# Two edits to the hand-set order of a streaming encoder layer: how many weight chunks may be split ahead at the end of the first feed-forward, and how many due pieces may run between two products in linear memory's heads

## The chip, the cores and the metric

The kernel runs on one core of a Trainium2 chip. The metric is the device time of one execution in microseconds (us); lower is better. The engines are named as in the profile: PE is TensorE (PEld its weight loads), DVE is VectorE, ACT is ScalarE, POOL is GpSimd, SP is SyncE, which issues most transfers.

## The reference

One layer of an encoder on 576 tokens: 512 of a new stream and 64 that continue a running one. D = 1024, feed-forward width 2816, four heads of matrix memory ("linear memory", mLSTM) of width 256, sixteen attention heads of width 64. All of it in f32.

```python
h = LN1(alpha*x + 0.5*FFN1(x))            # FFN: (silu(x@w_gate) * (x@w_up)) @ w_down
z = h @ w_in  -> mLSTM q,k,v,o,i,f | attention q,k,v | gates g_m, g_a
h = LN2(alpha*h + w_out(sig(g_m)*P_m(mLSTM(h)) + sig(g_a)*P_a(BandAttn(h))))
y = LN3(alpha*h + 0.5*FFN2(h))
# one mLSTM chunk, per head:
s   = (q k^T) * exp(dmat - m_t)
num = w_inter * (q C) + s v
h   = num / max(|w_inter * (q n) + sum(s)|, exp(-m_t))
C'  = decay*C + (w_s*k)^T v               # state; h is then normalised and gated by sig(o)
```

## The kernel before, in words

**Products.** Activations lie as 128 rows (features) by 576 columns (tokens), eight tiles for D. A weight chunk is 128 x 1024 f32: eight 128 x 128 blocks, one for each k tile. For f32 accuracy every operand is split into a rounded high part and a low part (the rest), and a product is three matmuls: wh·xh, wh·xl, wl·xh (`mm`, L132, is the one place where matmuls are issued; `transpose` is L142). The columns are taken in two halves. The `up`/`gate` products, most of the down product and the input projections run in a seven-product (Strassen-like) form; it is not touched here.

**Splitting a weight chunk.** `pump` loads a chunk into a raw buffer `wr` (two of them; SP, L246), copies it rounded on ACT into `wh` (`act`, L146) and subtracts on DVE into `wl` (`tt`, L149). There are four `wh` and four `wl` buffers (`NWB = 4`). The raw buffer comes free when the subtraction is done; a `wh`/`wl` pair comes free when the last matmul of its chunk is done. The chunks ("in",48), ("in",40) and ("in",32) are split in two pieces of 512 columns each. `plan` holds the order of all chunks; `take` marks the next chunk as in use (and splits it at once, if that has not happened), `done` gives it back. `pump` splits chunk c while c < taken + limit and while fewer than four chunks are split and not given back; it loads up to c + 1. `limit` is 2.

**The order of PE.** PE's instruction order is the order of the program text. A small queue, `Order`, puts the side work into it: `later(dt, fn)` enters a piece with a due time on a clock that advances with the estimated length of each matmul, and `tick`, called after each k step of a large product (three matmuls), runs every piece that is due. The calls of `pump` come from this queue too. The queues of ACT, DVE, POOL and SP are filled by the framework's scheduler: an instruction that is ready goes by its place in the program text, and `hot(n)` / `high_priority(offset=n)` moves it n places ahead. Each engine then runs its queue strictly in order.

**End of the first feed-forward** (`ffn`, n = 1). The last chunks of the plan are the seven-product chunks of output tiles 6 and 7, then four plain chunks: tile 6 with k 0 to 7 and with k 16 to 21, tile 7 with the same two (`plain`; called 6a, 6b, 7a, 7b below). They make the second column half (B) of tiles 6 and 7. Then come ("in",48), ("in",40), ("in",32), "if" (attention v, k, q of the first head pair and the memory's gate rows; called V0, K0, Q0, IF below) in one `gemm` with the passes `WAVE_M`: V0, K0 and Q0 together for the first half, IF for the first half, then the same for the second half. So the first k step of it needs three chunks split. Its right-hand side is the output of the layer norm `ln1`: `stats` (sums over features on PE: six narrow matmuls, one wide, six narrow; then `rsqrt` on POOL L491 and `dg` on DVE), `centre` (eight subtractions of the mean, `s<-s,c`, six on DVE, two on POOL), `spread` (one matmul, `aux<-dg,one`) and `apply` for each k tile (a scale on DVE L152, bias and rounding on ACT L146, low part on DVE L149), once for each half. `stats` of the first half is due while 6a runs, that of the second half soon after the `WAVE_M` product has begun.

**Linear memory's heads.** For each head `ml_kq` runs four projection chunks (k, k, q, q, with the causal convolution behind each) and enters the side work; `ml_early` enters the five score pieces (`weights`), `ml_late` the two `state` pieces, the five `hidden` pieces, `norm` and the two `back` transposes. So a head's pieces run between the k steps of the next head's projections, and those of the last head between four gate chunks (`FILL`). `turn5` transposes k or v (five transposes into two PSUM banks). v of the next head may only be turned when all five `hidden` pieces of this one have run; until then its piece enters itself again:

```python
            def v_turn(vf, sink):
                if hid[0] < 5 * h:
                    later(300, lambda: v_turn(vf, sink))
                else:
                    turn5(vf, sink)
```

All side work shares four PSUM banks with the tag `aux`. After the last head `od.drain()` runs what is left in the queue, one piece after the other, and the next products (`gate(7)`, then the projection `mp`) follow.

Of the kernel before, what the change touches and what calls it, by code (L numbers as in the profile page):

```python
# [45 lines left out]
class Order:  # L46


    def __init__(self):
        self.now = 0.0  # L50
        self.heap = []
        self.seq = 0
        self.bg = deque()
        self.bg_t = 0.0

    def later(self, dt, fn):
        self.seq += 1
        heapq.heappush(self.heap, (self.now + dt, self.seq, fn))
# [6 lines left out]
    def tick(self):  # L65
        while self.heap and self.heap[0][0] <= self.now:
            self.pop()
        while self.bg and self.bg_t <= self.now:
            self.bg_t = self.now + self.bg[0][0]
            if next(self.bg[0][1], self) is self:  # L70
                self.bg.popleft()
# [14 lines left out]
def tile_layer(ctx: ExitStack, tc: tile.TileContext, ins, outs):  # L86
# [3 lines left out]
    od = Order()  # L90
# [11 lines left out]
    def hot(off):  # L102
        def wrap(fn):
            def run(*a, **k):
                with tc.high_priority(offset=off):
                    return fn(*a, **k)
            return run
        return wrap

    def nm(s):  # L110
        uid[0] += 1
        return f"{s}_{uid[0]}"
# [11 lines left out]
    def f(ap):  # L124
        return ap.bitcast(F32)
# [19 lines left out]
    def act(out, in_, func=AF.Copy, **kw):  # L145
        return ACT.activation(out, in_, func, **kw)  # L146

    def tt(out, a, b, op, eng=None):
        return (eng or DVE).tensor_tensor(out, a, b, op=op)  # L149
# [18 lines left out]
    NWB = 4  # L168
# [15 lines left out]
    GR = 2150  # L184
    L_MEAN, L_STATS, L_SPREAD, L_SPREAD1 = 300, 1440, 4920, 3600
    plan = []
    wst = {"dma": 0, "conv": 0, "taken": 0, "used": 0, "stop": 0}
    raws, parts = {}, {}
    k0a, added = [], {}

    def add_lo(lo, hi, src):
        act(lo, f(hi), scale=-1.0)
        return POOL.dma_start(lo, src, accum_op=ALU.add)  # L193
# [31 lines left out]
        parts[c] = (hi, lo)  # L225

    @hot(30)
    def pump(limit=2):
        while True:
            c = wst["conv"]  # L230
            if wst["dma"] < len(plan) and plan[wst["dma"]][0] in EARLY + EARLY1:
                wst["dma"] += 1
                continue
            if c < len(plan) and plan[c][0] in EARLY + EARLY1:
                if c not in parts:
                    return
                wst["conv"] += 1
                continue
            if wst["dma"] < min(len(plan), c + 2):
                i = wst["dma"]  # L240
                if plan[i][1] is None:
                    wst["dma"] += 1
                    continue
                raws[i] = wpool.tile([P, 1024], F32, tag="wr", name=nm("wr"), bufs=2)
                src = plan[i][1]
                wst["load"] = SP.dma_start(raws[i][:, :src.shape[1]], src)  # L246
                wst["dma"] += 1
                continue
            if c < wst["stop"] and plan[c][0][0][:2] == "ds" and c < wst["taken"] + 4 and wst["used"] < NWB:
                split_ds(c)  # L250
                wst["used"] += 1
                wst["conv"] += 1
                continue
            if c < wst["stop"] and plan[c][0][0][:2] != "ds" and c < wst["taken"] + limit and wst["used"] < NWB:
                raw = raws.pop(c)
                n = plan[c][1].shape[1]
                hi = wpool.tile([P, 1024], F32R, tag="wh", name=nm("wh"), bufs=NWB)
                if plan[c][0] == "if":

                    r3 = raw[:, :n].rearrange("p (k c) -> p k c", c=64)  # L260
                    h3 = hi.rearrange("p (k c) -> p k c", c=P)
                    act(h3[:, :, 0:64], r3)
                    tt(h3[:, :, 64:128], r3, f(h3[:, :, 0:64]), ALU.subtract)
                    parts[c] = (hi, None)
                else:
                    lo = wpool.tile([P, 1024], F32R, tag="wl", name=nm("wl"), bufs=NWB)
                    step = n if plan[c][0] not in PIECES else 512
                    for a in range(0, n, step):

                        with tc.issue_after(k0a[0].ins) if plan[c][0] == ("in", 50) else nullcontext():  # L270
                            act(hi[:, a:a + step], raw[:, a:a + step])
                        if plan[c][0] in ADDED:
                            added[plan[c][0]] = add_lo(lo, hi, plan[c][1])
                            continue
                        before = wst.pop("behind", None)
                        with tc.issue_after(before.ins) if before is not None else nullcontext():
                            wst["lo"] = tt(lo[:, a:a + step], raw[:, a:a + step], f(hi[:, a:a + step]), ALU.subtract)
                    parts[c] = (hi, lo)
                wst["used"] += 1
                wst["conv"] += 1  # L280
                continue
            return

    def take(key):
        c = wst["taken"]
        assert plan[c][0] == key, (plan[c][0], key)
        wst["taken"] += 1
        if wst["conv"] <= c:
            pump(1)
        assert c in parts  # L290
        later(300, pump)
        return c
# [773 lines left out]
    def plain(n, ts_, hp, cs=(0, 2)):  # L1066

        for c in cs:
            k0, nk = DC[c]
            ids = {t: take((f"dn{n}", t, c)) for t, _ in ts_}  # L1070
            for i in range(nk):
                ww = slice(i * P, (i + 1) * P)
                for t, banks in ts_:
                    wh, wl = parts[ids[t]]
                    for ps, cc, new in banks:
                        xh, xl = hp.get(k0 + i, 0)
                        for w, x in ((wh, xh), (wh, xl), (wl, xh)):
                            mm(ps, w[:, ww], x[:, cc], new and k0 + i == 0 and w is wh and x is xh,
                               c == 2 and i == nk - 1 and w is wl, skip_group_check=True)
                    od.tick()  # L1080
            for t, _ in ts_:
                done(ids[t])
# [42 lines left out]
    def ffn(xs, n, gi, raw, final=None, prev=None):  # L1125
        hh = {}
        with tc.tile_pool(name=nm("hr"), bufs=FT, side="right", reuse_waits="tile") as hr, \
# [80 lines left out]
            with tc.tile_pool(name=nm("h1"), bufs=n1, side="right", reuse_waits="tile") as h1, \  # L1208
# [60 lines left out]
                if n == 1:  # L1269
                    ln.spread_at = L_SPREAD1  # L1270
                    for j in (6, 7):
                        ln.whole(j)
                    Y, V, W = bank()[:, :HT_], bank()[:, :HT_], bank("mm")[:, :HT_]
                    plain(n, ((6, ((Y, A, True),)),), hp_)
                    plain(n, ((7, ((V, A, True),)),), hp_)
                    ln.take(7, A, V, ALU.add)
                    Y, Z = seven(n, 6, inner, ln, Y)
                    ln.take(6, A, Y, ALU.add)
                    ln.last(6, A)
                    ln.last(7, A)  # L1280
                    plain(n, ((6, ((Z, B, False),)),), hp_)
                    ln.take(6, B, Z, ALU.add)
                    ln.last(6, B)
                    plain(n, ((7, ((W, B, True),)),), hp_)
                    ln.take(7, B, W, ALU.add)
                    ln.last(7, B)
                    HALVES[:] = HALVES_[0]
                else:
                    for hf in range(2):
                        ln.residual(6, hf)  # L1290
                    for j, hl in [(j, (hf,)) for hf in (0, 1) for j in (6, 7)]:
                        gemm([[((f"dn{n}", j, c), nk) for c, (_, nk) in enumerate(DC)]], hp_, [ln.cb(j)], (((0,), hl),))
# [94 lines left out]
    def out_cb(t, key, j):  # L1387
        def cb(hf, ps):
            with tc.issue_after(k0a[0].ins) if j == 1 and key == "v" else nullcontext():
                act(hs(t, hf), ps)  # L1390
            if hf == 1:
                SP.dma_start(outs[key][:, j, :], t)
        return cb
# [258 lines left out]
    for i, key in enumerate(EARLY1):  # L1652
        later(9000 + 4000 * i, lambda key=key: early(e1, key, EARLY1))
    gemm([[(("in", 48), KT)], [(("in", 40), KT)], [(("in", 32), KT)], [("if", KT)]], H,
         [out_cb(vf0, "v", 0), out_cb(kf0, "k", 0), q0_cb, gate_cb], WAVE_M)
    for i in range(4):
        combos.last = combos.add(i)
    ln1.close()
# [434 lines left out]
    def gate(j, pool, tag, func=AF.Copy):  # L2093
        s = sg[j] = slot(F32, pool, tag)
        gemm(one(("in", 56 + j)), H, [lambda hf, ps, s=s: act(hs(s, hf), ps, func)])

    for h in range(4):
        st = ml_kq(h)
        ml_early(h, st)
        ml_late(h, st)  # L2100
        for c in FILL[h]:
            gate(c - 56, *((sgp, "sg") if c < 60 else (None, "s")))
    del st
    od.drain()
    SP.dma_start(outs["conv"], conv_st)
    mstack.close()
# [150 lines left out]
```

## Time and profile before

| | |
|---|---|
| median of 3 runs | 1563.21 us (1562.77 to 1563.87) |
| profiled execution: its own time | 1562.92 us |
| profiled execution: span from first to last instruction | 1561.2 us |
| PE busy | 1542.1 us (99%) |
| DVE busy | 1144.0 us (73%) |
| ACT busy | 903.6 us (58%) |
| POOL busy | 206.3 us (13%) |
| mean granted TensorE clock | 0.995 |
| DMA | 208.13 MB, mean 133 GB/s |

The span is divided into stages in the order of the text: the first feed-forward until about 395 us, input projections until about 524 us, attention, then the heads of linear memory from about 859 to 1048 us, the projections and the second feed-forward. In the rows of the profile a number in brackets is the idle time of the engine just before an instruction, with what ended it; "x5" is five instructions of one kind that were merged into one row. `s` is the tag of most activation tiles, `c` the mean of a layer norm.

### The profile page before, as it was taken

How to read it: one execution, taken by the hardware profiler on the slowest of the kernel's cores; microseconds unless marked ns; L12 is line 12 of the kernel's file. 1: busy time of each engine (PE TensorE's matmuls, PEld its weight loads, DVE VectorE, ACT ScalarE, POOL GpSimd, SP SyncE). 2: the span in 40 equal slices, each digit the busy share in tenths (PEclk: the TensorE clock that was granted, in tenths of full speed). 3: DMA queues.
4: the chain of work that ended last, by engine and by line, in shares of the span. 5: the costliest groups of instructions: out<-in, count | busy, mean ns of one | idle time of the engine just before them, and what ended most of it. 6: DMA issues, size and time to landing. Idle time of an engine off the chain costs nothing.

```text
span 1561.2 us, 29480 instructions
## 1 busy us (share of the span) xinstructions
PE 1542.1 (99%) x11615; PEld 1526.5 (98%) x11615; DVE 1144.0 (73%) x2206; ACT 903.6 (58%) x1686; POOL 206.3 (13%) x391
## 2 busy tenths in 40 slices
PE   9999999999899999999999999999999999999998
PEld 9999999999899999999999999999999999999997
DVE  7777778686888677667686666755776777788766
ACT  7545457333766587777864877753456554557333
POOL 2000000000200143433201222202111000001000
PEclk9999999999899999999999999999999999999999
DMA  9322324533664376666534764643665222226334
GB/s 269 113 103 87 103 87 93 145 103 112 182 166 158 107 181 146 154 162 149 125 123 149 189 151 110 176 132 106 187 152 137 97 93 98 92 70 145 119 112 149
DMA packets 77731, 208.13 MB, mean 133 GB/s; under 512 B 8600, under 2 KB 20504, under 8 KB 77592
## 3 DMA queue, kind: packets, MB, share of 16 engines
q1 hardware_dynamic: 61464, 162.40, 31.3%
q0 software_dynamic: 12960, 38.02, 14.3%
q10 hardware_dynamic: 3168, 5.83, 1.1%
q8 instruction: 91, 1.49, 0.4%
q14 instruction: 48, 0.39, 0.1%
HBM read 174.56 MB, written 19.86 MB: 125 GB/s over the span
## 4 chain that ended last, share of the span: by engine, by line
PE 86%; DVE 5%; ACT 4%; DMA 2%; issue 1%; POOL 0%; SPq 0%; DVEq 0%; POOLq 0%; ACTq 0%
PE mm L132 71%; PE aux L132 14%; PE aux L142 2%; DVE s L149 1%; DVE sc L1530 1%; ACT wh L146 1%; DVE s L152 1%; ACT sc L146 0%; DMA wr<-in_w_dn 0%; ACT L146 0%; DVE wl L149 0%; DVE U L152 0%; DMA wr<-in_w_gu 0%; DMA w<-in_w_gu 0%; DMA s<-h 0%
## 5 line engine op out<-in xcount | busy, mean ns | idle before, releaser
L132 PE MATMUL mm<-s,wh 128*128 128x288 f32 (+2 forms) x3757 | 769.6, 298 | 2.3 <-ACT wh L146 1.0
L132 PEld LDWEIGHTS mm<-s,wh 128*128 128x128 f32 x3757 | 604.9, 190 | 5.2 <-ACT wh L146 1.2
L132 PE MATMUL mm<-s,wl 128*128 128x288 f32 (+2 forms) x1854 | 549.2, 296 | 3.4 <-DVE wl L149 3.4
L132 PEld LDWEIGHTS mm<-s,wl 128*128 128x128 f32 x1854 | 350.9, 189 | 3.6 <-DVE wl L149 3.6
L146 ACT ACTIVATE wh<-wr 128x1024 fp32r<-128x1024 f32 (+2 forms) x141 | 140.9, 1006 | 170.6 <-PE mm L132 101.0
L149 DVE TENSOR_TENSOR wl<-wr,wh 128x1024 fp32r<-128x1024 f32 (+2 forms) x95 | 109.9, 1165 | 51.3 <-ACT wh L146 51.2
L132 PE MATMUL mm<-tx,wh 128*128 128x288 f32 x635 | 131.3, 296 | 0.0
L132 PEld LDWEIGHTS mm<-tx,wh 128*128 128x128 f32 x635 | 102.2, 188 | 0.1
L149 DVE TENSOR_TENSOR wl<-wt,wh 128x1024 fp32r<-128x1024 f32 x48 | 58.7, 1224 | 52.8 <-ACT wh L841 52.8
L841 ACT ACTIVATE wh<-wt 128x1024 fp32r<-128x1024 f32 x48 | 50.8, 1059 | 80.2 <-DVE wt L149 79.2
L132 PE MATMUL mm<-tx,wl 128*128 128x288 f32 x326 | 96.1, 295 | 0.0
L149 DVE TENSOR_TENSOR wl<-wu,wh 128x1024 fp32r<-128x1024 f32 x60 | 73.4, 1223 | 28.9 <-ACT wh L841 28.9
L841 ACT ACTIVATE wh<-wu 128x1024 fp32r<-128x1024 f32 x60 | 63.4, 1057 | 36.2 <-PE mm L132 33.0
L132 PE MATMUL mm<-tx,ah 128*128 128x288 f32 x392 | 80.5, 297 | 0.0
L193 POOL DMA_DIRECT2D s<-s x16 | 13.7, 854 | 466.3 <-DVE hb L149 423.6
L146 ACT ACTIVATE h<-h 128x288 f32<-128x288 f32 x78 | 34.0, 436 | 59.9 <-DVE h L149 59.8
L132 PEld LDWEIGHTS mm<-tx,ah 128*128 128x128 f32 x392 | 62.4, 188 | 0.7 <-ACT c L146 0.4
L132 PE MATMUL mm<-h,wh 128*128 128x288 f32 (+2 forms) x304 | 62.7, 296 | 0.1
L149 DVE TENSOR_TENSOR wl<-ws,wh 128x1024 fp32r<-128x1024 f32 x48 | 58.5, 1219 | 4.0 <-ACT wh L841 4.0
L132 PEld LDWEIGHTS mm<-tx,wl 128*128 128x128 f32 x326 | 61.2, 188 | 0.0
L149 DVE TENSOR_TENSOR ws<-wu 128x1024 f32<-128x1024 f32 (+1 forms) x52 | 61.0, 1173 | 0.0
L132 PE MATMUL mm<-tx,al 128*128 128x288 f32 x196 | 57.6, 294 | 0.0
(394 smaller groups left out, 3488.0 us busy)
## 6 DMA issues: line engine op xcount, KB each, us to landing
wu<-in_w_gu SPq DMA_DIRECT2D x78, 512.0 KB, 4.3
wr<-in_w_in SPq DMA_DIRECT2D x54, 512.0 KB, 4.1
wl<-in_w_in POOLq DMA_DIRECT2D x42, 512.0 KB, 6.1
wr<-in_w_dn SPq DMA_DIRECT2D x38, 512.0 KB, 4.0
wu<-in_w_in SPq DMA_DIRECT2D x18, 512.0 KB, 4.8
wr<-in_w_dn SPq DMA_DIRECT2D x20, 384.0 KB, 3.7
s<-s POOLq DMA_DIRECT2D x16, 288.0 KB, 4.1
wu<-in_w_ap SPq DMA_DIRECT2D x8, 512.0 KB, 4.6
```

The lines of the kernel that those rows point to most:

```text
L132: PE.matmul(out, lhsT, rhs, start=start, stop=stop, **kw)
L142: PE.transpose(out, in_, idn)
L146: return ACT.activation(out, in_, func, **kw)
L149: return (eng or DVE).tensor_tensor(out, a, b, op=op)
L152: return DVE.scalar_tensor_tensor(out=out, in0=a, scalar=s, in1=b, op0=op0, op1=op1)
L193: return POOL.dma_start(lo, src, accum_op=ALU.add)
L841: self.last = ACT.activation(hi, src, AF.Copy)
L1530: DVE.tensor_tensor_reduce(out=out, in0=ps, in1=g, op0=ALU.add, op1=ALU.max, scale=1.0, scalar=-3e38, accum_out=acc)
```

## The change

`wst["ahead"]` takes the place of the constant 2 as `pump`'s limit. It is 2 everywhere except from the second column half of tile 6 in the first feed-forward (6a) until the `WAVE_M` product has been issued; there it is `NWB`, which is 4. And `Order` gets a switch, `single`: while it is set (the four heads, not the drain behind them), `tick` runs one due piece and leaves the rest to the next k steps. The earliest due piece goes first. Calls of `pump` and the repeated entries of `v_turn` count as pieces.

```diff
 class Order:
...
+        self.single = False
...
     def tick(self):
         while self.heap and self.heap[0][0] <= self.now:
             self.pop()
+            if self.single:
+                break
...
-    wst = {"dma": 0, "conv": 0, "taken": 0, "used": 0, "stop": 0}
+    wst = {"ahead": 2, "dma": 0, "conv": 0, "taken": 0, "used": 0, "stop": 0}
...
-    def pump(limit=2):
+    def pump(limit=None):
+        limit = limit or wst["ahead"]
         while True:
...
                     ln.take(6, A, Y, ALU.add)
                     ln.last(6, A)
                     ln.last(7, A)
+                    wst["ahead"] = NWB
                     plain(n, ((6, ((Z, B, False),)),), hp_)
...
     gemm([[(("in", 48), KT)], [(("in", 40), KT)], [(("in", 32), KT)], [("if", KT)]], H,
          [out_cb(vf0, "v", 0), out_cb(kf0, "k", 0), q0_cb, gate_cb], WAVE_M)
+    wst["ahead"] = 2
...
+    od.single = True
     for h in range(4):
         st = ml_kq(h)
         ml_early(h, st)
         ml_late(h, st)
         for c in FILL[h]:
             gate(c - 56, *((sgp, "sg") if c < 60 else (None, "s")))
     del st
+    od.single = False
     od.drain()
```

## The prediction

> **What bounds the kernel now.** First the page: the span, the engines, the granted clock.
>
> ```profile
> span 1561.2 us, 29480 instructions
> PE 1542.1 (99%) x11615; PEld 1526.5 (98%) x11615; DVE 1144.0 (73%) x2206; ACT 903.6 (58%) x1686; POOL 206.3 (13%) x391
> PEclk9999999999899999999999999999999999999999
> ```
>
> PE is busy for all but 19 us, so an edit of order can gain only where PE waits or runs slowly. One slice of forty, the eleventh (390 to 429 us), has a lowered clock. Next the waits of PE, over the span (total, times, longest):
>
> ```profile
> PE mm L132 <- DVE wl L149: 3.4, 1, 3.4
> PE aux L142 <- ACT hf L146: 1.8, 2, 0.9
> PE mm L132 <- ACT wh L146: 1.0, 1, 1.0
> PE aux L132 <- DVE og L152: 0.3, 1, 0.3
> ```
>
> Rows one and three are single waits for a weight split; two and four lie in the heads. The window view places them (length; busy time of PE, PEld, DVE, ACT, POOL with counts; clock; DMA):
>
> ```profile
> 396.00:398.00 2.00, 0.50 (x2) 0.30 (x2) 0.70 (x3) 2.00 (x5) 0.84 (x3) 1.00 1.06 379
> ...
> 402.00:404.00 2.00, 2.00 (x10) 1.86 (x9) 0.79 (x3) 0.00 (x0) 0.00 (x0) 0.50 0.73 254
> 404.00:406.00 2.00, 2.00 (x10) 1.86 (x9) 0.17 (x2) 0.79 (x3) 0.00 (x0) 0.50 0.64 252
> 406.00:408.00 2.00, 2.00 (x12) 2.00 (x11) 1.44 (x3) 1.94 (x5) 1.92 (x3) 0.50 0.05 18
> ...
> 410.00:412.00 2.00, 2.00 (x17) 1.89 (x16) 1.63 (x5) 0.58 (x1) 0.86 (x1) 1.00 0.93 234
> ```
>
> So at the first feed-forward's end PE waits 1.0 + 3.4 = 4.4 us, and then runs at half clock for some 8 us. The timeline says why, and how slow:
>
> ```profile
> 386.15 1.03 DVE L149 TENSOR_TENSOR dg<-ident,rs 128x256 f32<-128x256 f32 x1 [0.78 <-POOL rs L491]
> 386.26 1.16 ACT L146 ACTIVATE wh<-wr 128x512 fp32r<-128x512 f32 x2 [1.45 <-PE mm L132]
> ...
> 387.79 1.92 DVE L149 TENSOR_TENSOR s<-s,c 128x288 f32<-128x288 f32 x5
> ...
> 390.60 0.68 DVE L149 TENSOR_TENSOR wl<-wr,wh 128x512 fp32r<-128x512 f32 x1
> ...
> 391.31 0.33 SPq L246 DMA_DIRECT2D wr<-in_w_in  x1
> ...
> 394.63 0.40 PE L132 MATMUL mm<-s,wh 128*128 128x256 f32 x2
> ...
> 395.81 0.63 ACT L146 ACTIVATE wh<-wr 128x512 fp32r<-128x512 f32 x1 [1.70 <-DMA wr<-in_w_in]
> ...
> 399.68 0.68 DVE L149 TENSOR_TENSOR wl<-wr,wh 128x512 fp32r<-128x512 f32 x1
> ...
> 400.42 0.58 PE L132 MATMUL mm<-s,wl 128*128 128x256 f32 x1 [3.42 <-DVE wl L149]
> ...
> 407.52 0.63 PE L132 MATMUL mm<-s,wh 128*128 128x256 f32 x2
> 408.16 0.63 PE L132 MATMUL mm<-s,wh 128*128 128x256 f32 x2
> ...
> 409.27 0.40 PE L132 MATMUL mm<-s,wh 128*128 128x256 f32 x2
> ...
> 409.62 0.40 PE L132 MATMUL mm<-s,wh 128*128 128x256 f32 x2
> ```
>
> Read it backwards. PE, which began the three-chunk product at 394.63, stood until 400.42 for Q0's first low part (DVE, 399.68). Its high part was made at 395.81, when the load landed; from the high part (396.44) to the low part 3.2 us went by, in which DVE did layer-norm work queued ahead of it. The load went out at 391.31, the moment V0's second low part (390.60) gave the raw buffer back; and that stood behind the mean subtractions (387.79), though V0's high parts were done by 387.42. So a chain of three things is late: V0's low part, Q0's load, Q0's low part. Three matmuls of a k step take 0.64 us at half clock (407.52 to 408.16) and 0.35 us at full, from 409 on.
>
> **Part one, `ahead`.** It adds and removes no instruction and no byte; it changes where the text of the splits and loads stands. With limit 2, V0 is entered when 7a starts, K0 when 7b starts, Q0 when the product itself takes it. With limit 4 and four buffers, V0 is entered when 6a is given back, K0 when 6b is, Q0 when 7a is, IF when 7b is: each about one plain chunk sooner in the text. What that moves, chunk by chunk:
>
> 7a, 7b: entered sooner, but there are still four buffers and two raw ones; 0.
>
> V0's high part already runs at the instant that 6a's buffer is free (386.26, released by PE): 0. Its low part is now entered a few instructions after `centre`, within `pump`'s 30 places, so it can go ahead of the mean subtractions: at best as soon as `dg` is done and DVE turns to them, 387.8, and 1.9 us sooner than now. If only some of them are passed, 1 us. I take 1 to 1.9.
>
> Q0's load follows it: 389.4 to 390.3 in place of 391.31. The load took 395.81 - 391.31 = 4.5 us, so it lands at 393.9 to 394.8. One high and one low part (0.63, 0.68) then end at 395.2 to 396.1. PE wants the low part at 394.63 + 0.35 + 0.35 + 0.24 = 395.6. That leaves 0 to 0.5 us of the 4.4, if DVE takes the low part when it is ready. The text place of Q0 now lies ahead of the last `apply` steps; in the run it lay behind them.
>
> Price of passing: the subtractions that are passed start 1.3 us later (two low parts of 0.68). DVE does the same work in either order; if K0's low parts pass too, the first normalised k tile is late. Now it is just in time:
>
> ```profile
> 394.00 0.44 DVE L149 TENSOR_TENSOR s<-s,s 128x288 fp32r<-128x288 f32 x1
> ```
>
> It ends at 394.44, PE needs it at 394.75. A pair of low parts ahead of it would cost 1.0 us of waiting. This is what is late next: the layer norm on DVE. Its bound on the gain: from 394 to 412 the windows above show DVE idle for 1.30 + 1.21 + 1.83 + 0.56 + 0.37 = 5.3 us (it is full in those left out), and the second half has this slack:
>
> ```profile
> 414.24 0.82 DVE L149 TENSOR_TENSOR s<-s,s 128x288 fp32r<-128x288 f32 x2
> 416.64 0.31 PE L132 MATMUL mm<-s,wl 128*128 128x320 f32 x1
> ```
>
> Its first tile is done at 414.65, PE takes it up at 416.6: 2.0 us. With no idle DVE left, PE can reach the second half 7.3 us sooner, not more.
>
> The clock. PE resumed at 400.42 and was slow until some 409.0 (a k step that begins at 408.16 is slow, one at 409.27 is not), 8.6 us. In it lay the norm's sums, which took 3.4 us; the first half's, at full clock, took 1.8:
>
> ```profile
> 402.08 1.27 PE L132 MATMUL aux<-onec,s 128*128 128x1 f32 x6
> ...
> 405.45 0.77 PE L132 MATMUL mm<-s,wh 128*128 128x256 f32 x2
> ...
> 382.65 0.80 PE L132 MATMUL aux<-onec,s 128*128 128x1 f32 x6
> ...
> 384.46 0.51 PE L132 MATMUL mm<-hb,wh 128*128 128x288 f32 x2
> ```
>
> Loss: 1.6 on the sums and (8.6 - 3.4) x (1 - 0.35/0.64) = 2.4 on the rest, 4.0 us. It goes only if no long wait remains: waits of 0.9 us in the heads (below) stand in windows with clock 1.00.
>
> [...]
>
> So part one: at most 4.4 + 4.0 = 8.4 us, capped by DVE at 7.3. The norm keeps DVE waiting for POOL for some of that (0.78 us before `dg` in the first half, 386.15). I take 7.3 - 0.8 = 6.5 us; ends 0 and 8.4. SP: the loads of Q0 and IF may pass the `wu` loads that stand between them; `wu` is first used by the column products behind this stage, so that is covered.
>
> **Part two, `single`.** Same instructions again; PE's order changes. The two windows that hold most of the heads' idle time, and one of the waits:
>
> ```profile
> 880.00:910.00 30.00, 28.96 (x223) 28.20 (x223) 21.38 (x49) 25.21 (x59) 7.09 (x20) 1.00 0.75 197
> ...
> 985.00:1010.00 25.00, 24.04 (x193) 23.55 (x192) 17.92 (x54) 18.83 (x46) 5.97 (x17) 1.00 0.51 132
> ...
> 907.30 0.60 PE L142 MATMUL aux<-ident,qf 128*128 128x128 f32 x4
> 908.81 0.30 PE L142 MATMUL aux<-ident,qf 128*64 128x128 f32 x1 [0.91 <-ACT hf L146]
> ```
>
> With the 0.3 us that PE waits for `og`, 1.04 + 0.96 + 0.3 = 2.3 us. The stall at 908.81 ends a burst (last `hidden`, v turn, k turn, nothing between) that needed its fifth `aux` bank before ACT had emptied the first. With a k step (0.36 to 0.44 us) between the pieces two steps cover 0.8 of 0.91. I take 0.7 for each of the two such bursts and 0.1 of the third wait: 1.5 us; ends +2.3 and, for new waits that nothing here shows, -1.
>
> Delays that it adds: a piece waits one or two k steps, up to 0.9 us. `pump` waits too, but here splits wait for buffers, not for their text:
>
> ```profile
> ACT wh L146 <- PE mm L132: 13.5, 9, 3.4
> ```
>
> At the end of the heads the last `hidden` piece reaches ACT, the output is normalised on DVE (until 1046.72) and transposed on PE, 0.9 us later, so one or two steps are covered there.
>
> ```profile
> 1040.55 0.38 ACT L146 ACTIVATE hf<-aux 64x258 f32<-64x258 f32 x1 [1.57 <-PE aux L132]
> ...
> 1045.02 1.70 DVE L156 TENSOR_SCALAR hf<-hf,mv,mrs 128x256 f32<-128x256 f32 x5
> ...
> 1047.63 1.25 PE L142 MATMUL aux<-ident,hf 128*128 128x128 f32 x10
> ```
>
> Sum: 6.5 + 1.5 = 8.0 us off the profiled execution's 1562.92, 1554.9. The median of the runs is 0.29 above that execution: 1555.2.
>
> **Rivals.** (a) The stall shrinks but the clock still falls. If V0's low part stays behind the subtractions, Q0's load still lands at 395.75; high and low part end at 397.1, PE waits 1.5 us for them and about 1 us more for k tiles that ACT and DVE put behind. Of the 4.4 us 2.6 stay, and with them the 4.0: gain 1.8 + 1.5, 1559.9. For it: PE lost the clock at a time when it had been idle, but for two matmuls, only since 395.5. Against: V0's text passes `centre`.
>
> (b) It does not do what it says. V0 and K0 already wait for buffers, and a queue orders by readiness first, so the order on DVE could stay. Part two alone: 1561.7. Against: the 3.2 us that Q0's low part spent queued are order alone.
>
> (c) Slower, by part two. A `v_turn` that may not run enters itself again every 300 ns, and now each try takes the only place of a k step, so real pieces fall behind while it tries. If the last head's `hidden` pieces slip into the drain, no product covers the chain from the last of them to the transposes, 1040.55 to 1047.63, 7.1 us, and 4.0 us of half clock follow: 1563.2 - 6.5 + 11.1 = 1568. It turns the sign once the slip exceeds 0.9 us of slack by more than part one brings. Against: behind the last head no v waits, and 64 k steps stand for some 25 pieces.
>
> **How the numbers follow.** Forecast 0.64, own range 1553.6 to 1557.9 (part one 5.3 to 7.3, part two 0 to 2.3); (a) 0.16; (b) 0.12; (c) 0.08. The range takes in (a) with up to 1 us of new waits in the heads, and at the low end the full 8.4 + 2.3 = 10.7 us, should DVE not cap it: 1552 to 1561. It leaves out (b) and (c). No change that a measurement can tell is 0.2%, 3.1 us: faster means below 1560.1. Faster 0.64 + 0.11 of (a) = 0.75; same 0.05 + 0.12 = 0.17; slower 0.08.
>
> **What would show it.** Right: among PE's waits none for `wl` above 1 us, clock 1.00 in every window of that stretch, Q0's load out before 390.5, DVE nearly full from 394 to 405, and 2.0 us of slack at the second half gone. In the heads, `aux` pieces apart by at least one `mm` step and the two 0.9 us waits gone. Wrong: Q0's load still just after the subtractions, a wait for `s` in place of `wl`, a half-clock window, or `back` waiting for `hf` at the drain.

## The result, and the profile after

The changed kernel takes 1559.68 us (median of 10 runs, 1558.00 to 1562.51), the kernel before, on the same chip, 1563.26 (10 runs). The ratio is 0.9979, 95% interval 0.9970 to 0.9988: 3.6 us faster where 8.0 were forecast. Its profiled execution took 1559.54 us. First the page:

```profile
span 1557.8 us, 29488 instructions
PE 1539.1 (99%) x11615; PEld 1521.2 (98%) x11615; DVE 1143.0 (73%) x2206; ACT 903.4 (58%) x1686; POOL 205.4 (13%) x391
PEclk9999999999999999999999999999999999999999
```

The slice with the low clock is gone in this execution. Of PE's waits, those for `wl` (3.4) and `wh` (1.0) are gone at the boundary, and so are those for `hf` and `og` in the heads. In their place stand waits for `s`, the normalised tiles, and for `qk`, the split queries of a head's score product. The timeline of the changed kernel, the rows used below:

```profile
388.70 0.81 DVE L152 TENSOR_TENSOR s<-s,c 128x288 f32<-128x288 f32 x2
389.44 1.28 DVE L152 TENSOR_TENSOR wl<-wr,wh 128x512 fp32r<-128x512 f32 x2
...
390.74 0.33 SPq L250 DMA_DIRECT2D wr<-in_w_in  x1
...
394.44 0.63 ACT L149 ACTIVATE wh<-wr 128x512 fp32r<-128x512 f32 x1 [1.93 <-DMA wr<-in_w_in]
...
395.40 0.29 PE L135 MATMUL mm<-h,wl 128*128 128x288 f32 x1
396.31 0.38 PE L135 MATMUL mm<-s,wh 128*128 128x256 f32 x1 [0.62 <-ACT s L149]
397.07 0.38 PE L135 MATMUL mm<-s,wh 128*128 128x256 f32 x1 [0.38 <-DVE s L152]
...
399.30 0.38 PE L135 MATMUL mm<-s,wh 128*128 128x256 f32 x1 [0.89 <-DVE s L152]
...
404.33 0.40 PE L135 MATMUL mm<-s,wh 128*128 128x256 f32 x2
...
405.34 0.92 DVE L155 SCALAR_TENSOR_TENSOR s<-s,cols,aux 128x288 f32<-128x288 f32 x2
...
405.87 0.96 ACT L149 ACTIVATE s<-s,cols 128x288 f32<-128x288 f32 x2 [2.56 <-DVE s L155]
...
406.19 1.18 DVE L152 TENSOR_TENSOR s<-s,c 128x288 f32<-128x288 f32 x3
...
413.01 0.31 PE L135 MATMUL mm<-s,wl 128*128 128x320 f32 x1
...
873.61 1.28 ACT L149 ACT_TABLE_LOAD   x1
...
875.45 0.74 ACT L149 ACTIVATE vh<-aux 128x512 fp32r<-128x512 f32 x2
...
883.71 0.86 PE L135 MATMUL aux<-qk,s 128*128 128x512 f32 x3
...
884.35 0.70 ACT L149 ACTIVATE qk<-qf 128x576 fp32r<-128x576 f32 x1
...
885.10 0.50 PE L135 MATMUL aux<-qk,s 128*128 128x512 f32 x1 [0.52 <-ACT qk L149]
...
886.64 0.74 PE L135 MATMUL aux<-qk,s 128*128 128x512 f32 x2 [1.05 <-DVE qk L155]
...
1043.86 1.25 PE L145 MATMUL aux<-ident,hf 128*128 128x128 f32 x10
```

PE's order is the same in both kernels until the first head (874.56 in the kernel before), so the same matmul can be compared. Before, the last matmul of the first feed-forward stood here:

```profile
394.49 0.30 PE L132 MATMUL mm<-h,wl 128*128 128x288 f32 x1
```

The changed kernel is at that point 0.91 us later (395.40): a transfer at the start was late, by chance, for a second profile of the kernel before reaches this matmul at 393.68. The matmul that began at 409.62 before begins at 404.33: 5.3 us sooner, so the boundary has brought 6.2. At the second half (416.64 before, 413.01 after) 3.6 of the 5.3 us are left: 1.7 us were lost again. Some 0.65 us more go in the input projections: the matmul at 519.97 before begins at 516.99. At the score product of the first head (886.54 and 883.71) the changed kernel is 2.8 us ahead, at the last transposes of the heads (1047.63 and 1043.86) 3.8.

### The profile page after: what moved, and what is told of

Its sections match the earlier page's. It is cut to its first block, busy times and chain, and to the rows that moved or that the text cites. A ratio compares the mean times of both kernels' runs of the same rounds, so it can differ in the third digit from the quotient of the medians.

```text
span 1557.8 us, 29488 instructions
## 1 busy us (share of the span) xinstructions
PE 1539.1 (99%) x11615; PEld 1521.2 (98%) x11615; DVE 1143.0 (73%) x2206; ACT 903.4 (58%) x1686; POOL 205.4 (13%) x391
## 4 chain that ended last, share of the span: by engine, by line
PE 85%; DVE 7%; ACT 4%; DMA 2%; issue 2%; POOL 0%; SPq 0%; DVEq 0%; ACTq 0%; POOLq 0%
PE mm L135 69%; PE aux L135 13%; PE aux L145 2%; DVE wl L152 1%; DMA wr<-in_w_dn 1%; DVE U L155 1%; ACT wh L149 1%; DVE s L155 1%; ACT s L149 1%; DVE sc L1535 0%; DVE s L152 0%; ACT sc L149 0%; ACT L149 0%; DMA wr<-in_w_gu 0%; DMA w<-in_w_gu 0%
```

## The experiments

**Each part alone, on one chip.** The kernel before once more; `ahead` alone (`single` stays off); `single` alone (the limit stays 2); both.

> The kernel before once more, for a second profile of its start and its end. If the 1.0 us at the start (the wait for the transfer into s at 36 to 41 us) is chance, PE reaches 50 us anywhere from 0 to 1 us later than in the first profile. The boundary should repeat within 0.1 us: waits of 1.0 and 3.4 us and a half clock until 409.

> Part one alone: four chunks ahead at the end of the first feed-forward, all due pieces at once in the heads, as before. Theory S (the terms of the sum were mis-sized: the stage itself gives 4.4 us in the trace of the changed kernel, and 0.6 us of it go again in the stage behind it): 3.0 to 4.2 us faster than before, the heads' two waits of 0.9 us for hf still there. Rival N (the sizes were right, and that trace lost 1.0 us at its start and 0.5 at its end by chance): 5.5 to 6.5 us faster. Rival I (the parts help only together): under 2 us.

> Part two alone: one due piece at a time in the heads, two chunks ahead as before. Theory S: 0.5 to 1.2 us faster than before, with the wait of 3.4 us for wl and the half clock as before; the waits for hf are gone and waits for qk of 1.5 us stand in the first head in their place. Rival N: 1.5 to 2.2 us faster. Rival I: no gain or a loss.

> The changed kernel once more, for a second profile and a common chip. Theory S: 3.3 to 4.2 us faster than before, and in the trace the same waits for s and qk at the same places. Rival N: a start without the late transfer (PE not 1.0 us behind the kernel before at 50 us) and 4.5 to 5 us faster.

Measured, against 1562.86 (27 runs of before): `ahead` alone 1560.81, ratio 0.9985 (0.9976 to 0.9993); `single` alone 1562.96, 1.0000 (0.9992 to 1.0009); both 1559.62, 0.9982 (0.9973 to 0.9991). The one further run of the kernel before took 1561.17; PE's wait for `wh` was 0.4 us in it in place of 1.0, so the boundary did not repeat within the 0.1 us expected. So part one is worth some 2 us of its forecast 6.5, and part two by itself nothing of its 1.5: the first is below theory S, and for the second rival I held. The intervals reach some 1.4 us either way, so these runs do not show whether `single` adds anything on top of `ahead` (the medians differ by 1.2 us, the ratios by 0.5).

With `ahead` alone the runs fall in two groups by the mean clock: six with 0.998 or 0.999 average 1559.4 us, five with 0.995 to 0.997 average 1561.8. The kernel before has 0.994 to 0.997 in all of its runs. So the half clock must come back in part of the executions; profiles further below show it. The profile of the repeat with both edits shows where it can: windows of 3.41 us, as long as the half clock in it (887.07 to 890.48), laid so that the clock changes at their borders (length; PE, PEld, DVE, ACT, POOL busy; clock; DMA).

```profile
395.55:398.96 3.41, 2.13 (x15) 1.75 (x15) 3.41 (x9) 3.28 (x9) 1.69 (x4) 1.00 0.88 302
398.96:402.38 3.42, 3.42 (x30) 3.31 (x29) 2.21 (x7) 2.11 (x6) 0.97 (x2) 1.00 0.98 357
883.66:887.07 3.41, 1.83 (x10) 1.33 (x10) 3.38 (x6) 1.03 (x4) 1.07 (x3) 1.00 1.08 289
887.07:890.48 3.41, 3.41 (x14) 3.41 (x14) 1.60 (x3) 1.88 (x5) 0.00 (x0) 0.50 1.06 238
```

Here the window with 2.13 us of work is followed by full clock, the one with 1.83 by half clock. In this execution the two new waits for `qk` fell into one window, and 3.41 us at half clock followed; in the profile of the changed kernel above they did not.

**Is it the order of DVE? Three edits of the queue.** First, the scale steps of the first half's k tiles 4 to 7 ahead of the second half's norm:

```diff
-            stt(dh, dh, g, rb, ALU.mult, ALU.mult)
+            with tc.high_priority(offset=HOT) if self.gi == 0 and hf == 0 and j >= 4 else nullcontext():
+                stt(dh, dh, g, rb, ALU.mult, ALU.mult)
```

> Theory: in the changed kernel 1.8 of the 6.2 us that the boundary gains are lost again between 406 and 414 us, because DVE's queue holds the second half's norm (dg, six subtractions of the mean) ahead of the first half's last scale steps, and ACT stands 2.56 us for them. With the scale steps of k tiles 4 to 7 of the first half moved ahead, that wait of ACT and PE's gaps at 407 to 409 go, and PE reaches the second half 1 to 1.8 us sooner: 1558.3 median (from 1559.6). Rival: DVE is full from 404 to 412 whatever its order, so what is passed (the second half's subtractions) makes the second half late by as much: 1559.6, no difference from the changed kernel.

1563.51, ratio 1.0004 (0.9995 to 1.0013): all of the gain is gone, which neither the theory nor the rival had. Timeline of that kernel:

```profile
394.12 1.78 DVE L155 SCALAR_TENSOR_TENSOR s<-s,cols,aux 128x288 f32<-128x288 f32 x4
...
398.56 0.40 PE L135 MATMUL mm<-s,wh 128*128 128x256 f32 x1 [3.46 <-DVE s L152]
```

The scale steps now went ahead of the first k tile's low part as well, and PE waited 3.46 us for it. What is gained behind is lost in front: this edit does not tell what the 1.7 us are worth.

Second, the low parts of V0's and K0's second 512 columns on POOL, and that together with the first edit and the next one:

```diff
-    tt(lo[:, a:a + step], raw[:, a:a + step], f(hi[:, a:a + step]), ALU.subtract)
+    tt(lo[:, a:a + step], raw[:, a:a + step], f(hi[:, a:a + step]), ALU.subtract,
+       POOL if a and plan[c][0] in (("in", 48), ("in", 40)) else None)
```

> After the change, with the low parts of the second 512 columns of V0 and K0 subtracted on POOL (idle from 388.8 to 395.2 us) in place of DVE. Theory: DVE's work sets the waits left at the start of the three-chunk product (0.62 + 0.38 + 0.89 us) and, through them, how often the clock falls. DVE has 2 x 0.64 = 1.3 us less to do there, so the waits shrink by 1 us or more and fewer executions lose the clock: 1557.8 median. Rival: Q0's load sets them; POOL takes longer for a subtraction than DVE (0.87 against 0.45 us for 128x288), the raw buffer comes free later, and the waits stay or grow: 1559.6 to 1561.

> All three edits on top of the change: scale steps of the first half's k tiles 4 to 7 ahead, only pieces with matmuls counted, second low parts of V0 and K0 on POOL. Theory: the gains stand in three places and add: 1.3 + 2.3 + 1.8 = 5.4 us, 1554.2 median, clock 0.998 or more in nearly all executions. Rival, DVE full and one piece per step too slow: 1559.6.

1561.68 (0.9993, 0.9984 to 1.0002) and 1561.50 (0.9990, 0.9981 to 0.9999): both lose most of the change's gain, more than the rivals said. Timeline of the POOL edit alone:

```profile
388.31 1.90 DVE L152 TENSOR_TENSOR s<-s,c 128x288 f32<-128x288 f32 x2
388.32 1.58 POOL L152 TENSOR_TENSOR wl<-wr,wh 128x512 fp32r<-128x512 f32 x1
...
390.14 0.68 DVE L152 TENSOR_TENSOR wl<-wr,wh 128x512 fp32r<-128x512 f32 x1
```

POOL needs 1.58 us for V0's second piece where DVE needs 0.64, but it is done at 389.90 and not the late one. Beside it the two mean subtractions on DVE take 1.90 us (0.81 in the changed kernel), and V0's first piece, which DVE does behind them, ends at 390.82; Q0's load goes out at 390.88. ACT could split Q0 only at 395.61 in place of 394.44. Most of that is the load, which kept ACT waiting until 4.7 us after its start in place of 3.7; why is not shown.

**Pieces without matmuls do not count.** In the heads `tick` stops only after a piece that issued matmuls:

```diff
+            t = self.now
             self.pop()
-            if self.single:
+            if self.single and self.now > t:
                 break
```

> After the change, but in the heads tick stops only after a piece that issued matmuls; pump calls and v turn's repeated entries no longer take the place of a k step. Theory: these empty pieces delayed the first head's v turn by three k steps, ACT's split of v and of qk slipped behind, and PE got new waits for qk of 0.52 + 1.05 us, which in some executions also bring half clock. Without them: no wait for qk above 0.3 us, clock 1.00 between 880 and 895 us, 1.6 to 3 us faster than the changed kernel, 1557.3 median. Rival: one real piece per k step is too slow in itself, so the qk waits stay: 1559.6.

> The kernel that counts only pieces with matmuls, once more, as the base of the next three. Theory: its boundary is the changed kernel's, three waits of 0.6, 0.4 and 0.9 us, after which the clock stays at 1.00 in some executions and falls to 0.50 for some 8 us in others, at a price of 2.5 to 3 us: times spread over 1556 to 1560.6, mean clock 0.999 in the fast ones and 0.996 in the others. Rival: the clock's fall in the earlier profile belongs to that one execution, and nearly all runs lie together.

1559.19 (0.9973, 0.9962 to 0.9984), and in the repeat 1558.04 (0.9969, 0.9958 to 0.9981); the changed kernel had 0.9979 and 0.9982, with intervals that overlap these. The waits for `qk` are gone, but the clock still falls at the boundary in part of the executions. Timeline of the repeat; it runs 2.0 us behind the changed kernel at this place (its score product starts at 885.68):

```profile
396.12 0.38 PE L136 MATMUL mm<-s,wh 128*128 128x256 f32 x1 [0.58 <-ACT s L150]
396.88 0.39 PE L136 MATMUL mm<-s,wh 128*128 128x256 f32 x1 [0.38 <-DVE s L153]
...
399.10 0.58 PE L136 MATMUL mm<-s,wh 128*128 128x256 f32 x1 [0.89 <-DVE s L153]
...
415.67 0.31 PE L136 MATMUL mm<-s,wl 128*128 128x320 f32 x1
...
874.88 0.63 ACT L150 ACTIVATE vh<-aux 128x512 fp32r<-128x512 f32 x1
...
876.20 1.28 ACT L150 ACT_TABLE_LOAD   x1
...
884.15 0.68 ACT L150 ACTIVATE qk<-qf 128x576 fp32r<-128x576 f32 x1
```

ACT splits v ahead of its table load here; in the changed kernel the v turn came three k steps later, ACT had gone on to the table load (873.61), and `qk` followed at 884.35, which is 2.2 us later when the 2.0 are taken off. In the first head `v_turn` never enters itself again (`hid[0] < 5 * h` cannot hold when `h` is 0), so what took the k steps there were calls of `pump` or other pieces without matmuls, such as `decays`; which of them is not shown.

Its boundary is the same program as the changed kernel's, with the same three waits (0.58, 0.38, 0.89), yet it ran at half clock. Windows of that execution:

```profile
395.37:398.78 3.41, 1.88 (x12) 1.31 (x10) 3.41 (x9) 2.97 (x8) 2.56 (x6) 1.00 0.96 314
398.78:402.20 3.42, 3.10 (x13) 2.95 (x14) 2.55 (x6) 1.49 (x4) 0.00 (x0) 0.50 0.92 370
402.20:405.61 3.41, 3.41 (x17) 3.27 (x16) 1.00 (x3) 1.79 (x5) 1.27 (x2) 0.50 0.51 184
405.61:409.02 3.41, 3.41 (x18) 3.41 (x18) 3.41 (x9) 1.19 (x3) 1.29 (x2) 0.50 0.00 0
409.02:412.44 3.42, 3.42 (x28) 3.31 (x28) 3.42 (x10) 3.42 (x6) 0.78 (x1) 1.00 0.37 105
```

and of the changed kernel's profile:

```profile
393.46:396.88 3.42, 2.61 (x18) 2.18 (x16) 3.29 (x8) 2.44 (x6) 1.52 (x4) 1.00 0.81 211
396.88:400.29 3.41, 2.33 (x18) 2.12 (x18) 3.41 (x9) 3.14 (x8) 1.38 (x3) 1.00 0.90 330
400.29:403.70 3.41, 3.41 (x28) 3.31 (x28) 2.21 (x6) 1.79 (x5) 1.34 (x2) 1.00 1.01 377
```

In these profiles a half clock lasts whole windows of 3.41 us: one in the repeat with both edits (887.07 to 890.48), three in the kernel before (398.80 to 409.04, 10.24 us) and here (398.78 to 409.02). In the changed kernel's profile a border fell between the waits (396.88, with 2.61 and 2.33 us of work beside it), and the clock stayed up; here one window held nearly all of them (1.88), and it fell, for three windows. The price is 2.85 us: from the first wait's end to the first `wl` matmul of the second half 415.67 - 396.12 = 19.55 here, 413.01 - 396.31 = 16.70 there.

**Can the waits be made short enough?** On top of the last kernel: the second low parts of K0 and Q0 on POOL (V0's stay on DVE, so Q0's load is not held up); Q0's first 512 columns loaded with V0 into a free activation slot; both.

```diff
+       POOL if a and plan[c][0] in (("in", 40), ("in", 32)) else None)
...
+                if plan[i][0] == ("in", 48):
+                    wst["first"] = slot(F32)[:, :512]
+                    wst["load"] = SP.dma_start(raws[i][:, :src.shape[1]], src)
+                    SP.dma_start(wst["first"], plan[i + 2][1][:, :512])
+                elif plan[i][0] == ("in", 32):
+                    wst["load"] = SP.dma_start(raws[i][:, 512:], src[:, 512:])
```

> On top of counting only pieces with matmuls: the low parts of the second 512 columns of K0 and Q0 (needed only from k tile 4 on) on POOL. V0's stay on DVE, so Q0's load goes out as before. Theory: the waits for the low parts of k tiles 0 and 1 (0.38 and 0.89 us) are DVE's queue; with 0.64 us taken away before the first and 0.64 us more before the second they shrink to 0.3 us together; the first wait (0.62, ACT stands for Q0's load) stays. 1 us from that, and fewer executions lose the clock: 1557.5 median. [...]

> On top of counting only pieces with matmuls: Q0's first 512 columns are loaded into a free activation slot together with V0's chunk, not into a raw buffer that V0's low part must give back; the second 512 columns come as before. Theory: ACT no longer stands 1.9 us for Q0's load with the first k tile's steps behind it, so the first wait of 0.62 us goes and the ones after it shrink: 0.6 to 1 us, and fewer executions lose the clock, 1557.8 median. Rival: DVE's queue alone sets when the first k tiles are done: 1559.2.

> Both: Q0's first half loaded early, second low parts of K0 and Q0 on POOL, only pieces with matmuls counted. Theory: less than 0.6 us of waits is left at the start of the three-chunk product, no execution loses the clock there, 1.5 us of waits and the 2.5 to 3 us of half clock that some executions paid are gone: 1556 median, clock 0.998 or more. Rival: 1559.2.

1557.19 (0.9967, 0.9954 to 0.9979), 1558.87 (0.9974, 0.9964 to 0.9983) and 1556.49 (0.9958, 0.9945 to 0.9972), against 1558.04 for their base; the intervals overlap. The early load alone brings nothing: in its profile the waits are 0.25, 0.53 and 1.15 us, and the clock fell. The POOL edit alone has 0.41, 0.50 and 0.29. With both, the timeline is

```profile
395.96 0.39 PE L136 MATMUL mm<-s,wh 128*128 128x256 f32 x1 [0.44 <-DVE s L153]
397.77 0.39 PE L136 MATMUL mm<-s,wh 128*128 128x256 f32 x1 [0.48 <-DVE s L153]
398.93 0.83 PE L136 MATMUL aux<-onec,s 128*128 128x1 f32 x6 [0.30 <-DVE s L153]
```

1.2 us of waits in place of 1.9 (the expectation had less than 0.6), and the same 1.2 as with the POOL edit alone: the early load is not needed. All five runs have a mean clock of 0.998 or 0.999. A fall of three windows would take 0.003 off the mean (half of 10.24 us in 1556), so it is ruled out; a fall of one window, at 0.001, is not. The three waits that are left are all for DVE. The windows of that execution:

```profile
398.75:402.17 3.42, 3.24 (x25) 3.14 (x26) 2.40 (x7) 2.22 (x7) 2.21 (x5) 1.00 1.02 401
402.17:405.58 3.41, 2.81 (x22) 2.41 (x20) 3.14 (x6) 1.20 (x4) 2.10 (x3) 1.00 0.27 109
```

**The two terms by themselves.** The heads' edit alone in the form that counts only matmuls (limit 2), the boundary's three edits alone, and all once more.

> Kernel before with the heads' edit alone, in the form that counts only pieces with matmuls (limit stays 2). Theory: the forecast's 1.5 us for part two was right for the mechanism and was eaten by the empty pieces: without them the two waits of 0.9 us for hf go, no wait for qk comes, and it gains 1 to 2 us: 1561.3 median against 1562.8 before. Rival: order in the heads is worth nothing in any form, since what is late is ACT's and DVE's work: 1562.8.

> The boundary's three edits alone (limit 4, Q0's first half loaded early, second low parts of K0 and Q0 on POOL), the heads as before. Theory: it holds the 6.2 us of the boundary less what is given back at the second half, without any execution at half clock there: 4.3 to 5 us, 1558.3 median, clock 0.998 or more in all. Rival: the clock still falls in part of the executions, as in the kernel with limit 4 alone: 1560.8, clock 0.995 to 0.999.

> The kernel with both (boundary's three edits, only pieces with matmuls counted in the heads) once more. Theory: the two parts add: 1558.3 - 1.5 = 1556.8, and again no execution below a mean clock of 0.998. Rival: the earlier five executions were lucky, and some lose the clock: 1558 with clocks of 0.995 to 0.999.

Against 1563.07 (16 runs of before): heads 1560.70, ratio 0.9988 (0.9979 to 0.9998); boundary 1559.05, 0.9970 (0.9959 to 0.9982), its clock 0.998 or 0.999 in all six runs; all 1556.91, 0.9961 (0.9949 to 0.9974). The parts add: 2.4 + 4.0 = 6.4 against 6.2. The profile of the heads alone, whose rows before are 886.54 and 1047.63,

```profile
885.44 1.57 PE L136 MATMUL aux<-qk,s 128*128 128x512 f32 x6
...
1044.73 1.25 PE L146 MATMUL aux<-ident,hf 128*128 128x128 f32 x10
```

is 1.1 us ahead at the first and 2.9 at the second: the heads bring 1.8. One of the five last runs has a clock of 0.997, which the expectation ruled out, and the profile of that kernel, from a run with 0.998, shows a fall of one window:

```profile
397.06:400.47 3.41, 3.10 (x22) 2.79 (x23) 2.88 (x8) 1.86 (x6) 2.35 (x6) 1.00 0.99 350
400.47:403.88 3.41, 3.41 (x18) 3.41 (x17) 2.65 (x6) 2.18 (x6) 2.81 (x3) 0.50 0.65 264
403.88:407.30 3.42, 3.42 (x29) 3.31 (x28) 3.42 (x9) 1.94 (x4) 0.04 (x1) 1.00 0.42 149
```

So the fall is shorter but not gone. It cost nothing by the second half: from the end of the first feed-forward to the first `wl` matmul of the second half PE takes 17.1 us here, and 17.1 or 17.2 in the three profiles that have the same POOL pieces and no fall.

This version beats both kernels of the case: 0.9958 and 0.9961 against 0.9979 and 0.9982 for the change as it was made; the ends of the intervals overlap a little.

## Why the prediction was wrong

**What held.** V0's low part passed mean subtractions, though only the last three of DVE's six (389.44 behind 388.70). Q0's load went out at 390.74, which is 1.5 us sooner when the late start of 0.91 is taken off; the forecast had 1.0 to 1.9. The waits for `wl` and `wh` went. DVE is full from 396 to 400 and the first half's last steps are what is late next. In the heads the waits for `hf` and `og` went. In the profiled execution 6.2 us came of the stall and the clock together, where at most 8.4 were counted and 6.5 taken.

How much of it lasts can be read from the same matmuls of PE in all profiles. From the end of the first feed-forward to the second half PE takes 21.4 to 22.3 us in four profiles with limit 2; with limit 4 it takes 17.6 or 17.7 in three whose clock stayed up there, and 20.4 and 20.5 in two where it fell for three windows. To the matmul at 519.97 it takes 124.7 to 125.7, then 121.6, and 123.8 and 123.9. So part one brought some 3.6 us where the clock stayed up and some 1.4 where it fell, and two steps failed.

**Where part one failed: "It goes only if no long wait remains".** The step took the clock's fall for a matter of one long wait, and the forecast said that 0 to 0.5 us of waiting would be left. 1.9 us were left, in three waits of at most 0.9. That each is short did not help: with 1.88 us of work left in one 3.41 us window half clock followed, with 2.61 and 2.33 on the two sides of a border it did not, and where the borders lie differs from execution to execution (396.88 in the one, 395.37 and 398.78 in the other). So rival (a) was true in part of the executions, at 2.85 us each, and not in the others. The median of `ahead` alone (2 us) lies between: with the waits cut to 1.2 us and no fall of three windows in any run (the boundary's edits alone) it is 4.0. That the result is near rival (a)'s 1559.9 is chance: the part two that this rival counted on brought nothing by itself.

**The second failed step: the cap, 7.3 - 0.8.** It is the larger one, for even with the clock up the boundary gives 3.6 us and not 6.5. It counted idle DVE time up to the second half as if all but 0.8 could be used. In the changed kernel DVE was still idle for 1.2 us between 400 and 404 (busy 1.43 and 1.37 of 2.00 us in the two halves of that stretch), where it mostly stands for the results of the sums. Of the 6.2 us 1.7 were given back before the second half began: in DVE's queue the last scale steps of the first half (405.34) come so late that ACT had stood 2.56 us for them (405.87), and the second half's mean subtractions (406.19) follow before their low parts. That this order is the cause is argued from the timeline; the edit that should have shown it moved too much. That PE is not what sets the second half's start is borne out by the last kernel, where a window at half clock ahead of it cost nothing. Some 0.65 us more go by 520 us; their cause stays open.

**Part two.** The size was right: 1.5 us forecast, 1.8 in the profile and 2.4 (0.3 to 3.3 by the interval) in the median of the heads' edit once only pieces with matmuls count. What was missed is that empty pieces take k steps too: the first head's v turn slips, and PE waits 0.52 + 1.05 us for `qk`, with half clock behind it in some executions. From the matmul that begins at 857.97 before to the last transposes of the heads PE takes 189.3 to 189.7 us in four profiles with the heads as before; with the change as made 188.6 and 188.7 in two where the clock stays up, and 190.2 to 191.0 in three where it falls behind the waits for `qk`; and 187.5 to 187.9 in eight where only pieces with matmuls count. So the change as made gains or loses by the clock, and the median of `single` alone shows nothing. Rival (c) came near this mechanism, but it spoke of the tries of `v_turn` and of the drain; it was other empty pieces, in the first head. The forecast's lower end for new waits, -1, was too small.

The 8.6 us that the prediction read from the k steps lie in three whole windows, in the kernel before (0.50 from 398.80 to 409.04, 10.24 us) as in the rows above (0.50 from 398.78 to 409.02). In the kernel before PE had 0.61 us of work in the window ahead of the fall (395.39 to 398.80); 1.88 us of work in it, in the rows above, did not prevent the fall.

## What to carry to other kernels

Add PE's waits up over stretches of 3.41 us, the length of the shortest half clock seen here, and do not judge them one by one: three waits of under 1 us cost 2.85 us in clock in one profile here, more than the 1.9 of waiting, and nothing in another with the same boundary, so read the mean clock of every run beside its time before a median is explained by one profile. When a limit of one piece per slot is put on a queue, let only pieces that use the slot count. And when splits are moved ahead of a norm, ask which pieces in that queue are needed only later: two of them given to an idle engine helped here (1.2 us of waits in place of 1.9), but not the one whose buffer the next load was waiting for.

## What was unexpected of the hardware

A window that was busy all through did not always bring the clock back: in the repeat of the kernel that counts only pieces with matmuls PE was busy from 402.20 to 405.61 for 3.41 of 3.41 us, and the next window was still at half clock. In that window and the one before lie the norm's sums, narrow matmuls of one column (six from 400.34, six from 402.57); in the third, 405.61 to 409.02, lie only wide ones, and the clock came back after it. The table of the last kernel has a fall behind such sums: 3.10 us busy, with the sums in it, and half clock follows. Whether the narrow matmuls count for less is not shown: no run tried it by itself, and the window from 398.75 to 402.17 (the early load with the POOL edit), with the same sums in it and 3.24 us busy, was followed by full clock.

Busy time does not settle it without sums either. In the tables above, windows without sums and with 1.83 or 1.88 us of work were followed by half clock, those with 2.13 or 2.61 by full clock, but the profile of the three queue edits together has one with 1.81 that was followed by full clock:

```profile
395.51:398.92 3.41, 1.81 (x13) 1.39 (x11) 3.41 (x8) 2.96 (x7) 2.86 (x8) 1.00 0.56 171
398.92:402.34 3.42, 1.58 (x12) 1.38 (x12) 3.25 (x8) 2.94 (x8) 0.00 (x0) 1.00 0.90 310
```

An estimate that fits better counts columns, the second number of a shape such as 128x256, over the matmuls that start in a window; a narrow matmul adds one. In the profiles of the kernel before and of the changed kernel, between 20 and 1540 us, the windows with 512, 1794 and 842 columns (from 395.39, 398.80 and 402.22 in the kernel before) were followed by half clock and all others, which have 3465 or more, by full clock. Elsewhere half clock followed 2560 columns (from 395.37, the repeat of the kernel that counts only pieces with matmuls) and 3072 (from 883.66, the repeat with both edits). Where the line lies, and why, is not shown, and no run tried it by itself.
